# The variance of differential attention outputs by float32 products, and a second buffer for the second map's exponentials

## The chip, the cores and the metric

One core of one Trainium2 chip runs the whole kernel in one launch. The core has five queues that matter here: TensorE (matrix products, in the trace PE, with its weight loads shown apart as PEld), VectorE (DVE), ScalarE (ACT), GpSimd (POOL) and the queue that issues most transfers (SP). The metric is device time in microseconds (us), the median over runs. Before the change three runs gave 897.48, 897.6 and 898.41 us, median 897.6.

## The reference, cut to what matters

The block takes 1024 tokens of width 1024. One RMS-normalised input feeds two attention branches; the change lies in the first, differential attention with 4 heads and two score maps per head:

```python
o_diff = causal_multimap_attention(dq, dk, dv, weights, DIFF_HEAD_DIM ** -0.5)   # weights = [1, -lam]
o_diff = rms_norm(o_diff, diff_subln[layer]) * (1.0 - lambda_init)
o_diff = o_diff.transpose(0, 2, 1, 3).reshape(b, s, DIFF_WIDTH)
o_diff = o_diff * jax.nn.silu(dgate)

def rms_norm(x, gain):
    y = xf * lax.rsqrt(jnp.mean(xf * xf, axis=-1, keepdims=True) + NORM_EPS)
    return y * gain
```

So each head's 128 output values of a token are divided by the root of their mean square. That mean square is the variance of the title. The second branch (MLA, multi-head latent attention) has one score map per head; both branches are projected, gated, added, projected again and normalised.

## The kernel before, in words

All matrix products of the projections and of attention are done in three products of split operands (`mm3`, lines 159 to 162: high by high, high by low, low by high), each 512 columns wide where it can be. The work runs in five stages: the input products into values and latents (to about 130 us), the differential heads with the gate projections mixed in (130 to 574 us), a handover in which the MLA heads are prepared (574 to 600 us), MLA attention (to about 725 us), and the output products (to the end).

A differential head goes through two groups of four query blocks (`diff_head`, line 684). For each block `diff_scores` (line 608) makes two score tiles on TensorE (line 619); `softmax` (line 433) finds the row maximum on VectorE (line 435) and takes the exponential with its sum on ScalarE (line 438), the first map into tile `e0` to `e7`, the second into tile `eb`. `combine` (line 623) then weighs and subtracts the second map on VectorE (line 627). `eb` has one buffer, so the next block's second exponential may not start before line 627 has read the last one.

`values` (line 446) transposes the probabilities on TensorE, splits them, and gathers `ov`, a tile with the head's 128 values on the partitions and 512 tokens along the row. `diff_norm` (line 630) runs once for each group, 8 times in all:

- ScalarE squares `ov` into the float32 tile `sq` (line 632; its buffer has the tag `rt1`, and traces show it as `rt`).
- VectorE splits `sq` into three bfloat16 parts by four instructions (lines 642 to 645), and makes the gated, unnormalised output `o` (line 646).
- `variance` (line 648) makes the sum over the partitions on TensorE: for each 128 tokens three products with `parts` as the weights and `meanw`, two columns of 1/128, as the moving operand (line 652). That is 12 loads of weights and 12 products for each group, 96 in all.
- VectorE adds the epsilon (`ve`, line 654), GpSimd takes the power -1/2 (`rv`, line 656), and `diag` and `finish` spread the result over the partitions by two more products (lines 671, 672), multiply and store it.

In the last group (head 3, second half) the tiles `parts`, `o` and the diagonals lie in `e4` to `e7`, since that group falls into the handover. There TensorE works on the rope part of the MLA queries (two groups of nine products with `wqnh`) and on the MLA values (eight groups of six products with `wvh`). Each of these groups fills one of two `mm` PSUM buffers in turn: a query group's is free again when VectorE has read it twice (`rotate`, lines 487 and 488; 489 and 490 go on in SBUF), a value group's when ScalarE has copied it (`mvh`) and VectorE has written the remainder (`mvl`, line 153). `q_stack` (lines 493 to 498) then splits the rotated queries into `mqs` on ScalarE (line 496) and VectorE (line 498).

The order in the queues has two sources. The Python code issues filler work between the steps (`fill`, `defer`), and when the program is built a scheduler places each engine's instructions by priority and readiness; waits between engines are then added. Within a queue an instruction that waits holds all behind it.

Of the kernel before, what the change touches and what calls it, by code (L numbers as in the profile page):

```python
# [14 lines left out]
F32 = mybir.dt.float32  # L15
F32R = mybir.dt.float32r
BF16 = mybir.dt.bfloat16
I32 = mybir.dt.int32
AF = mybir.ActivationFunctionType
ALU = mybir.AluOpType  # L20
# [3 lines left out]
P = 128  # L24
S = 1024
# [26 lines left out]
def emit(tc, a):  # L52
    nc = tc.nc
    V, A, G, T = nc.vector, nc.scalar, nc.gpsimd, nc.tensor

    def pool(name, side=None, space=None, bufs=1):
        kw = {}
        if side:
            kw["side"] = side
        if space is not None:  # L60
            kw["space"] = space
        return tc.alloc_tile_pool(name=name, bufs=bufs, reuse_waits="tile", **kw) if space is not DRAM \
            else tc.alloc_tile_pool(name=name, bufs=bufs, **kw)
# [3 lines left out]
    def nm(s):  # L67
        counter[0] += 1
        return f"{s}_{counter[0]}"

    def mk(p, shape, dt, tag, bufs=None):
        return p.tile(shape, dt, name=nm(tag), tag=tag, bufs=bufs)

    def one(p, shape, dt, name):
        return p.tile(shape, dt, name=name, tag=name, bufs=1)
# [9 lines left out]
    def tick(ns):  # L85
        clock[0] += ns
        while later and clock[0] >= later[0][0]:
            heapq.heappop(later)[2]()
# [35 lines left out]
    const = pool("const", "left")  # L124
# [12 lines left out]
    ones = one(const, [P, P], F32, "ones")  # L137
    onesr = one(const, [P, P], F32R, "onesr")
    ident = one(const, [P, P], F32, "ident")
    meanw = one(const, [P, 2], BF16, "meanw")  # L140
    nhalf = one(const, [P, NB], F32, "nhalf")
    halfpi = one(const, [P, 1], F32, "halfpi")
    rstd = one(const, [P, NB], F32, "rstd")
# [23 lines left out]
    def blk(b):  # L167
        return slice(b * P, b * P + P)
# [233 lines left out]
    wk = pool("wk", "left")  # L402
# [15 lines left out]
    def chunks(W):  # L418
        if W == 640:
            return [(0, 384), (384, 256)]  # L420
        out, c = [], 0
        while c < W:
            n = min(512, max(256, W - c))
            out.append((c, n))
            c += n
        return out

    def scores_tile(W):

        sc = mk(ps, [P, S], F32, "sc", 2)  # L430
        return sc[:, P:S] if W == 640 else sc

    def softmax(sc, W, scale, dst):
        mn = mk(wk, [P, 1], F32, "mn", 4)
        V.tensor_tensor_reduce(sc[:, 0:W], sc[:, 0:W], mask[:, S - W:S], scale=-scale, scalar=BIG,  # L435
                               op0=ALU.add, op1=ALU.min, accum_out=mn)
        sm = mk(wk, [P, 1], F32, "sm", 8)
        A.activation(dst, sc[:, 0:W], AF.Exp, scale=-1.0, bias=mn, accum_out=sm)  # L438
        return sm

    def recip(sm):
        r = mk(wk, [P, 1], F32, "rs", 8)
        V.reciprocal(r, sm)  # L443
        return r
# [60 lines left out]
    later_pools = {}  # L505
# [102 lines left out]
    def diff_scores(h, i):  # L608
        qh, ql, kh, kl = stacks[h]
        W = (i + 1) * P  # L610
        ea = mk(wk, [P, W], F32, f"e{i}", 1)
        eb = mk(later_pools["st"], [P, S], F32, "eb", 1)
        sc = [scores_tile(W) for m in range(2)]

        for c0, n in chunks(W):
            for x, (q, k) in enumerate(((qh, kh), (qh, kl), (ql, kh))):
                for m in range(2):
                    r = slice(64 * m, 64 * m + 64)
                    T.matmul(sc[m][:, c0:c0 + n], lhsT=q[r, blk(i)], rhs=k[r, c0:c0 + n], start=x == 0, stop=x == 2)  # L619
            tick(3 * n * ROW)  # L620
        sums = [softmax(sc[m], W, DIFF_SCALE, e[:, 0:W]) for m, e in enumerate((ea, eb))]

        def combine():
            r1, r2 = recip(sums[0]), recip(sums[1])
            V.tensor_scalar(r2, r2, nlam, None, op0=ALU.mult)
            V.tensor_scalar(ea, ea, r1, None, op0=ALU.mult)
            V.scalar_tensor_tensor(ea, eb[:, 0:W], r2, ea, op0=ALU.mult, op1=ALU.add)
        return ea, combine

    def diff_norm(h, g, ov):  # L630
        sq = mk(wk, [P, 512], F32, "rt1", 2)
        A.activation(sq, ov, AF.Square)
        if (h, g) != (3, 1):
            parts = [mk(p1c, [P, 512], BF16, f"sq{i}", 1) for i in range(3)]
            o = mk(p1c, [P, 512], F32, "o", 1)
            dg = [mk(p1c, [P, 512], F32R, x, 1) for x in ("rt1r", "rt2r")]
        else:
            spare = [mk(wk, [P, (i + 1) * P], F32, f"e{i}", 1) for i in range(4, 8)]
            parts = spare[3].bitcast(BF16)
            parts = [parts[:, 512 * i:512 * i + 512] for i in range(3)]  # L640
            o, dg = spare[0][:, 0:512], [x[:, 0:512].bitcast(F32R) for x in spare[1:3]]
        V.tensor_copy(parts[0], sq)
        V.tensor_tensor(sq, sq, parts[0], op=ALU.subtract)
        V.tensor_copy(parts[1], sq)
        V.tensor_tensor(parts[2], sq, parts[1], op=ALU.subtract)
        V.scalar_tensor_tensor(o, ov, gsub, dgate[h, g], op0=ALU.mult, op1=ALU.mult)

        def variance():
            vb = bank_n()
            for j in range(4):  # L650
                for i in range(3):
                    T.matmul(vb[:, 2 * j:2 * j + 2], lhsT=parts[i][:, blk(j)], rhs=meanw, start=i == 0, stop=i == 2)
            ve = mk(wk, [P, 8], F32, "ve", 2)
            V.tensor_scalar(ve, vb[:, 0:8], EPS, None, op0=ALU.add)
            rv = mk(wk, [P, 4], F32, "rv", 2)
            G.tensor_tensor(rv, ve.rearrange("p (a b) -> p a b", b=2)[:, :, 0], nhalf[:, 0:4], op=ALU.pow)
            defer(2500, lambda: diag(rv))

        def diag(rv):
            rh = mk(wk, [P, 4], F32R, "rvh", 2)  # L660
            rl = mk(wk, [P, 4], F32R, "rvl", 2)
            V.tensor_copy(rh, rv)
            V.tensor_tensor(rl, rv, f32(rh), op=ALU.subtract)
            for x, t in zip((rh, rl), dg):
                (V if (h, g) == (3, 1) and t is dg[1] else G).tensor_tensor(t.rearrange("p (a b) -> p a b", b=P), ident.unsqueeze(1).broadcast_to([P, 4, P]),
                                f32(x).unsqueeze(2).broadcast_to([P, 4, P]), op=ALU.mult)
            defer(6000, finish)

        def finish():
            bb = bank_n()  # L670
            T.matmul(bb, lhsT=onesr, rhs=dg[0], start=True, stop=False)
            T.matmul(bb, lhsT=onesr, rhs=dg[1], start=False, stop=True)
            V.tensor_tensor(o, o, bb, op=ALU.mult)
            nc.sync.dma_start(d_od[h][:, half(g)], o)

        defer(6000, variance)
# [4 lines left out]
    def bank_n():  # L681
        return mk(ps, [P, 512], F32, "tp", 1)
# [130 lines left out]
    p1c = later_pools["c"]  # L813
# [179 lines left out]
    parts = {}  # L993
# [169 lines left out]
    for i, c in enumerate(quarters):  # L1163
# [8 lines left out]
        else:  # L1172
            sq = mk(p3d, [P, 256], F32, "sq3", 1)
# [86 lines left out]
```

## Time and profile before

| | |
|---|---|
| median of three runs | 897.6 us (897.48 to 898.41) |
| the profiled execution: its time, its span | 896.13 us, 894.4 us |
| TensorE busy | 874.7 us, 98% of the span |
| VectorE, ScalarE, GpSimd busy | 538.5, 335.5, 219.5 us |
| TensorE's mean granted clock | 0.995 of full speed |

The span is the stretch from the first to the last instruction; 1.7 us of the execution lie around it. A busy share of 98% on TensorE is not work at its peak: products are pipelined, their recorded ends overlap the next start, and a product of two columns counts as busy for 163 ns. What an operation costs TensorE is therefore read from start to start.

### The profile page before, as it was taken

The page shows a single profiled execution, that of the slowest core. Times are in us where ns is not written, and L with a number is a line of the kernel's source. Part 1 is how long each engine was busy: PE and PEld are TensorE (multiplying, and loading weights), DVE is VectorE, ACT ScalarE, POOL GpSimd, SP SyncE. Part 2 cuts the span into 40 slices and gives each one's busy share as a digit, 9 for nine tenths or more (in the row PEclk, how much of TensorE's full clock was granted, in tenths as well). Part 3 has the DMA queues.
Part 4 walks back from the last instruction along what each step waited for, and adds up shares of the span by engine and source line. Part 5 has one row for each costly group of instructions (what it writes and reads, how often), then busy time and mean ns, then how long its engine had stood idle before and what let it go on. Part 6 is the DMA issues. An engine that isn't in the chain of part 4 may idle for free.

```text
span 894.4 us, 11691 instructions
## 1 busy us (share of the span) xinstructions
PE 874.7 (98%) x4368; PEld 716.0 (80%) x4368; DVE 538.5 (60%) x1023; ACT 335.5 (38%) x654; POOL 219.5 (25%) x163
## 2 busy tenths in 40 slices
PE   9989999999999999999999999999999999999997
PEld 6879988787887878878778778778877788888886
DVE  5472348738368483784856755786676775561432
ACT  5651361334323343233422333745455542221211
POOL 2432013222223222322223131622313212210001
PEclk9998999999999999999999999999999999999999
DMA  8765026122131222222211215410104655434151
GB/s 294 289 192 161 23 87 220 48 71 80 62 107 59 76 90 64 91 71 82 72 59 33 95 31 185 161 34 25 48 25 154 200 178 187 141 102 146 58 178 47
DMA packets 48824, 96.71 MB, mean 108 GB/s; under 512 B 4992, under 2 KB 17536, under 8 KB 48768
## 3 DMA queue, kind: packets, MB, share of 16 engines
q1 hardware_dynamic: 46176, 89.81, 30.4%
q0 software_dynamic: 1152, 3.67, 1.3%
q10 hardware_dynamic: 1440, 2.49, 0.8%
q8 instruction: 34, 0.56, 0.3%
q14 instruction: 22, 0.18, 0.1%
HBM read 68.96 MB, written 27.00 MB: 107 GB/s over the span
## 4 chain that ended last, share of the span: by engine, by line
PE 85%; DVE 4%; DMA 4%; issue 2%; ACT 2%; POOL 1%; SPq 1%; POOLq 0%; DVEq 0%; ACTq 0%
PE mm L160 18%; PE mm L162 17%; PE mm L161 17%; PE sc L619 4%; PE acc L160 3%; PE acc L161 3%; PE acc L162 3%; PE tp L457 2%; PE bank L161 2%; PE bank L160 2%; PE bank L162 2%; PE pv L161 2%; PE pv L160 2%; PE pv L162 1%; PE sc L898 1%
## 5 line engine op out<-in xcount | busy, mean ns | idle before, releaser
L160 PE MATMUL mm<-hh,wh 128*128 128x512 f32 x512 | 205.9, 402 | 0.0
L162 PE MATMUL mm<-hh,wl 128*128 128x512 f32 x512 | 200.2, 391 | 0.0
L161 PE MATMUL mm<-hl,wh 128*128 128x512 f32 x512 | 199.9, 390 | 0.0
L153 POOL TENSOR_TENSOR wl<-wr,wh 128x1024 fp32r<-128x1024 f32 x32 | 81.8, 2558 | 240.2 <-ACT wh L152 240.2
L160 PEld LDWEIGHTS mm<-hh,wh 128*128 128x128 f32 x512 | 96.2, 188 | 25.0 <-issue 3.8
L162 PEld LDWEIGHTS mm<-hh,wl 128*128 128x128 f32 x512 | 96.1, 188 | 21.2
L161 PEld LDWEIGHTS mm<-hl,wh 128*128 128x128 f32 x512 | 96.3, 188 | 17.9
L438 ACT ACTIVATE e<-sc,mn 128x128 f32<-128x128 f32 (+3 forms) x64 | 47.5, 743 | 82.9 <-DVE mn L435 80.0
L435 DVE CUSTOM_DVE_ANT_0 sc<-sc,mask 128x128 f32<-128x128 f32 (+7 forms) x96 | 71.7, 774 | 10.1 <-PE sc L902 8.7
L153 DVE TENSOR_TENSOR pl<-tp,ph 128x512 fp32r<-128x512 f32 (+2 forms) x52 | 31.5, 606 | 62.2 <-ACT ph L152 62.2
L152 ACT CAST ph<-tp 128x512 fp32r<-128x512 f32 (+2 forms) x52 | 27.0, 520 | 84.7 <-PE tp L457 84.2
L160 PE MATMUL acc<-woh,mh 128*128 128x512 f32 (+1 forms) x136 | 51.7, 380 | 0.0
L162 PE MATMUL acc<-woh,ml 128*128 128x512 f32 (+1 forms) x136 | 51.7, 380 | 0.0
L161 PE MATMUL acc<-wol,mh 128*128 128x512 f32 (+1 forms) x136 | 51.7, 380 | 0.0
L152 ACT CAST wh<-wr 128x1024 fp32r<-128x1024 f32 x32 | 33.6, 1050 | 39.0 <-PE mm L161 28.6
L160 PE MATMUL bank<-wch,hh 128*128 128x384 f32 (+1 forms) x128 | 42.7, 335 | 3.8 <-ACT wch L152 3.8
L911 POOL TENSOR_TENSOR e<-e,rs 128x128 f32<-128x128 f32 (+5 forms) x24 | 24.9, 1042 | 73.5 <-DVE rs L443 73.4
L161 PE MATMUL bank<-wcl,hh 128*128 128x384 f32 (+1 forms) x128 | 42.6, 333 | 0.3 <-DVE wcl L153 0.3
L569 DVE TENSOR_TENSOR g<-mm,rbc 128x512 f32<-128x512 f32 x40 | 27.5, 688 | 25.5 <-PE mm L162 25.0
L162 PE MATMUL bank<-wch,hl 128*128 128x384 f32 (+1 forms) x128 | 42.4, 331 | 0.0
L153 POOL TENSOR_TENSOR wpl<-wpr,wph 128x512 fp32r<-128x512 f32 x16 | 22.0, 1377 | 68.0 <-ACT wph L152 68.0
L572 ACT ACTIVATE u<-g 128x512 f32<-128x512 f32 x40 | 25.2, 630 | 20.3 <-DVE g L569 15.4
(291 smaller groups left out, 1859.0 us busy)
## 6 DMA issues: line engine op xcount, KB each, us to landing
wr<-in_w_t SPq DMA_DIRECT2D x32, 512.0 KB, 3.5
d_t<-u SPq DMA_DIRECT2D x32, 256.0 KB, 2.0
tg<-d_t SPq DMA_DIRECT2D x32, 256.0 KB, 3.0
big<-in_x SPq DMA_DIRECT2D x8, 512.0 KB, 8.3
wor<-in_w_out SPq DMA_DIRECT2D x8, 512.0 KB, 4.5
xres<-in_x SPq DMA_DIRECT2D x8, 512.0 KB, 5.1
big<-in_xT SPq DMA_DIRECT2D x7, 512.0 KB, 6.6
craw<-d_c SPq DMA_DIRECT2D x5, 512.0 KB, 6.0
```

The lines of the kernel that those rows point to most:

```text
L152: A.copy(hi, src)
L153: (eng or V).tensor_tensor(lo, src, f32(hi), op=ALU.subtract)
L160: T.matmul(ps, lhsT=lh, rhs=rh, start=first, stop=False)
L161: T.matmul(ps, lhsT=lh, rhs=rl, start=False, stop=False)
L162: T.matmul(ps, lhsT=ll, rhs=rh, start=False, stop=last)
L435: V.tensor_tensor_reduce(sc[:, 0:W], sc[:, 0:W], mask[:, S - W:S], scale=-scale, scalar=BIG, op0=ALU.add, op1=ALU.min, accum_out=mn)
L438: A.activation(dst, sc[:, 0:W], AF.Exp, scale=-1.0, bias=mn, accum_out=sm)
L457: T.transpose(tp[:, blk(j)], probs[j][:, blk(kb)], ident)
L569: V.tensor_tensor(g, b, rbc[:, half(n)], op=ALU.mult)
L572: A.activation(u, g, AF.Tanh, scale=0.5 / by)
L619: T.matmul(sc[m][:, c0:c0 + n], lhsT=q[r, blk(i)], rhs=k[r, c0:c0 + n], start=x == 0, stop=x == 2)
L911: G.tensor_tensor(e, e, r.broadcast_to([P, W]), op=ALU.mult)
```

## The change

The squares go to TensorE as they are, in float32. For each 128 tokens one float32 product takes the place of three bfloat16 products, `meanw` becomes a float32 tile, and the four splitting instructions and their tiles are gone. Besides, `eb` gets a second buffer.

```diff
-    meanw = one(const, [P, 2], BF16, "meanw")
+    meanw = one(const, [P, 2], F32, "meanw")
...
     ea = mk(wk, [P, W], F32, f"e{i}", 1)
-    eb = mk(later_pools["st"], [P, S], F32, "eb", 1)
+    eb = mk(later_pools["st"], [P, S], F32, "eb", 2)
...
     A.activation(sq, ov, AF.Square)
     if (h, g) != (3, 1):
-            parts = [mk(p1c, [P, 512], BF16, f"sq{i}", 1) for i in range(3)]
             o = mk(p1c, [P, 512], F32, "o", 1)
             dg = [mk(p1c, [P, 512], F32R, x, 1) for x in ("rt1r", "rt2r")]
         else:
-            spare = [mk(wk, [P, (i + 1) * P], F32, f"e{i}", 1) for i in range(4, 8)]
-            parts = spare[3].bitcast(BF16)
-            parts = [parts[:, 512 * i:512 * i + 512] for i in range(3)]
+            spare = [mk(wk, [P, (i + 1) * P], F32, f"e{i}", 1) for i in range(4, 7)]
             o, dg = spare[0][:, 0:512], [x[:, 0:512].bitcast(F32R) for x in spare[1:3]]
-        V.tensor_copy(parts[0], sq)
-        V.tensor_tensor(sq, sq, parts[0], op=ALU.subtract)
-        V.tensor_copy(parts[1], sq)
-        V.tensor_tensor(parts[2], sq, parts[1], op=ALU.subtract)
         V.scalar_tensor_tensor(o, ov, gsub, dgate[h, g], op0=ALU.mult, op1=ALU.mult)

         def variance():
             vb = bank_n()
             for j in range(4):
-                for i in range(3):
-                    T.matmul(vb[:, 2 * j:2 * j + 2], lhsT=parts[i][:, blk(j)], rhs=meanw, start=i == 0, stop=i == 2)
+                T.matmul(vb[:, 2 * j:2 * j + 2], lhsT=sq[:, blk(j)], rhs=meanw, start=True, stop=True)
```

On TensorE, in the first head's sixth block of scores, before (three of the twelve products; `sc` are the score tiles, `tp` the PSUM tile of the variance):

```order
L619 MATMUL sc_1967<-kh_1421,ql_1420 128x512
L652 LDWEIGHTS sq_337_1899
L652 MATMUL tp_1974<-meanw,sq_337_1899 128x2
L652 LDWEIGHTS sq_338_1900
L652 MATMUL tp_1974<-meanw,sq_338_1900 128x2
L652 LDWEIGHTS sq_339_1901
L652 MATMUL tp_1974<-meanw,sq_339_1901 128x2
```

and now (`rt` is the tile of squares; a float32 product loads its weights itself and has no row for it):

```order
L619 MATMUL sc_1959<-kh_1421,ql_1420 128x512
L619 MATMUL sc_1960<-kh_1421,ql_1420 128x512
L644 MATMUL tp_1967<-meanw,rt_336_1897 128x2 x4
L619 MATMUL sc_1959<-kh_1421,qh_1419 128x256
L619 MATMUL sc_1960<-kh_1421,qh_1419 128x256
```

The place among the neighbours is the same, here and in the other six groups before the handover; twelve loads and products became four instructions.

On VectorE in the handover, before (`e` and `rt` the parts and the squares, `rt` with `mm` the rotated queries, `mvl` the remainders of MLA values, `ve` the variance with epsilon):

```order
L643 TENSOR_TENSOR rt_1116_5328<-rt_1116_5328,e_1120_5333 128x512
L487 STREAM_SHUFFLE rt_1132_5398<-mm_5387 128x512
L644 CAST e_1120_5333<-rt_1116_5328 128x512
L488 TENSOR_TENSOR rt_1131_5397<-mm_5387,cosm 128x512
L645 TENSOR_TENSOR e_1120_5333<-rt_1116_5328,e_1120_5333 128x512
L489 TENSOR_TENSOR rt_1132_5398<-rt_1132_5398,sinm 128x512
L153 TENSOR_TENSOR mvl_5352<-mm_5407,mvh_5345 128x512
L490 TENSOR_TENSOR rt_1131_5397<-rt_1131_5397,rt_1132_5398 128x512
L153 TENSOR_TENSOR mvl_5353<-mm_5416,mvh_5346 128x512
L654 TENSOR_SCALAR ve_5458<-tp_5445 128x8
L498 TENSOR_TENSOR mqs_1128_5385<-rt_1131_5397,mqs_1128_5385 64x512
L498 TENSOR_TENSOR mqs_1129_5386<-rt_1131_5397,mqs_1129_5386 64x512
```

and now (`rvh` is the rounded result of GpSimd's power; the lines after the diff's are 7 or 8 lower than before):

```order
L639 SCALAR_TENSOR_TENSOR e_1096_5225<-pv_5022,gsub,du_4390 128x512
L487 STREAM_SHUFFLE rt_1110_5288<-mm_5277 128x512
L488 TENSOR_TENSOR rt_1109_5287<-mm_5277,cosm 128x512
L489 TENSOR_TENSOR rt_1110_5288<-rt_1110_5288,sinm 128x512
L646 TENSOR_SCALAR ve_5340<-tp_5335 128x8
L490 TENSOR_TENSOR rt_1109_5287<-rt_1109_5287,rt_1110_5288 128x512
L153 TENSOR_TENSOR mvl_5242<-mm_5297,mvh_5235 128x512
L654 CAST rvh_5363<-rv_5342 128x4
L498 TENSOR_TENSOR mqs_1106_5275<-rt_1109_5287,mqs_1106_5275 64x512
L498 TENSOR_TENSOR mqs_1107_5276<-rt_1109_5287,mqs_1107_5276 64x512
L153 TENSOR_TENSOR mvl_5243<-mm_5306,mvh_5236 128x512
L655 TENSOR_TENSOR rvl_5364<-rv_5342,rvh_5363 128x4
```

The splitting is gone from between the rotation's steps, `ve` and `rvh` moved forward, and the second `mvl` moved back behind `rvh` and both `mqs`.

On GpSimd, ahead of the heads, the scheduler now puts the first two loads of the differential values (lines 603, 604) ahead of one split of weights (line 153); on SP the two loads of line 605 stand ahead of a store and a load that they followed before.

## Rows read from the trace of the kernel before

**Rows 1.** The page: busy us of each engine, its share and its instructions.

```profile
PE 874.7 (98%) x4368; PEld 716.0 (80%) x4368; DVE 538.5 (60%) x1023; ACT 335.5 (38%) x654; POOL 219.5 (25%) x163
```

**Rows 2.** TensorE's waits, 130 to 574 us, then 574 to 598 us (total, times, longest).

```profile
PE tp L457 <- DVE pl L153: 1.4, 1, 1.4
...
PE mm L160 <- DVE mvl L153: 1.5, 1, 1.5
PE tp L672 <- DVE e L665: 0.5, 1, 0.5
```

**Rows 3.** Durations by line in ns (min/median/max): variance, then the last float32 product.

```profile
L652 PEld LDWEIGHTS <-sq x84: 95/96/100, 209.1 to 529.5; 128*128 128x128 bf16 x84
L474 PEld LDWEIGHTS pv<-plast,dvf x16: 187/188/192, 200.9 to 574.1; 128*128 128x128 f32 x16
L474 PE MATMUL pv<-plast,dvf x16: 270/273/274, 201.1 to 574.2; 128*128 128x128 f32 x16
```

**Rows 4.** Timeline of TensorE, a group between scores (start us, us; xN merges N).

```profile
209.08 0.45 PE L652 MATMUL tp<-meanw,sq 128*128 128x2 bf16 x12
209.46 0.39 PE L619 MATMUL sc<-kh,qh 64*128 64x256 f32 x2
```

**Rows 5.** Timeline of TensorE, a group between products of a projection.

```profile
263.14 0.39 PE L162 MATMUL mm<-hh,wl 128*128 128x512 f32 x1
263.37 0.45 PE L652 MATMUL tp<-meanw,sq 128*128 128x2 bf16 x12
263.68 0.48 PE L160 MATMUL mm<-hh,wh 128*128 128x512 f32 x1
264.01 0.39 PE L161 MATMUL mm<-hl,wh 128*128 128x512 f32 x1
```

**Rows 6.** Timeline of TensorE, one float32 product between products of a projection.

```profile
256.10 0.40 PE L162 MATMUL mm<-hh,wl 128*128 128x512 f32 x1
256.33 0.39 PE L474 MATMUL pv<-plast,dvf 128*128 128x128 f32 x2
256.79 0.39 PE L161 MATMUL mm<-hl,wh 128*128 128x512 f32 x1
```

**Rows 7.** Tile eb: ScalarE's idle time before its exponentials (us, times).

```profile
  DVE mn L435: 0.8, 4
```

**Rows 8.** Timeline of the handover, all engines.

```profile
576.14 0.40 PE L162 MATMUL mm<-ch,wqnl 128*128 128x512 f32 x1
577.90 3.23 POOL L153 TENSOR_TENSOR krl<-u,krh 128x512 fp32r<-128x512 f32 x2
578.83 1.17 DVE L645 TENSOR_TENSOR e<-rt,e 128x512 bf16<-128x512 f32 x1
579.93 1.76 DVE L489 TENSOR_TENSOR rt<-rt,sinm 128x512 f32<-128x512 f32 x1
581.61 0.68 DVE L153 TENSOR_TENSOR mvl<-mm,mvh 128x512 fp32r<-128x512 f32 x1
582.34 0.50 PE L160 MATMUL mm<-ch,wqnh 128*128 128x512 f32 x1 [1.49 <-DVE mvl L153]
582.98 1.26 ACT L496 CAST mqs<-rt 64x512 fp32r<-64x512 f32 x2 [1.74 <-DVE rt L490]
583.63 1.41 DVE L498 TENSOR_TENSOR mqs<-rt,mqs 64x512 fp32r<-64x512 f32 x2
583.64 1.54 POOL L656 TENSOR_TENSOR rv<-ve,nhalf 128x4 f32<-128x4 f32 x1 [2.50 <-DVE ve L654]
...
597.53 0.49 PE L457 MATMUL mm<-ident,e 128*128 128x128 f32 x3
```

**Rows 9.** Line 489 by itself: ns of one (min/median/max).

```profile
L489 DVE TENSOR_TENSOR rt<-rt,srs x16: 677/682/2655, 144.4 to 484.0; 128x512 f32<-128x512 f32 x16
```

**Rows 10.** Timeline of GpSimd and of the SP queue ahead of the heads.

```profile
138.10 0.32 SPq L528 DMA_DIRECT2D d_c<-rt  x1
138.35 2.40 POOL L153 TENSOR_TENSOR wl<-wr,wh 128x1024 fp32r<-128x1024 f32 x1 [14.82 <-ACT wh L152]
```

## The prediction, made before the changed kernel ran

> **What bounds the kernel now.** I read the busy shares first: TensorE is busy for 874.7 of 894.4 us, VectorE for 538.5 [rows 1]. A change that takes work off VectorE is thus worth only what TensorE waits for VectorE, and a change that adds to TensorE is paid in full where nothing holds TensorE up. So the second view is TensorE's own waits, by stage. From 130 to 574 us, where seven of the eight variance groups lie, it waits for VectorE once, 1.4 us, for the remainder of a transposed tile (line 153) and not for the variance; in the handover it waits 1.5 us for the remainder `mvl` and 0.5 us for a diagonal [rows 2]. Third, the timeline of TensorE around a variance group, from start to start, because the recorded busy time of so short products overlaps.
>
> **What the group of products costs now.** Between scores, the twelve bfloat16 loads and products begin at 209.08 and the next score product at 209.46: 0.38 us [rows 4]. Between products of a projection, 0.87 us pass from the start at 263.14 to the start at 264.01 [rows 5]; two products of 512 columns lie in it, each 0.23 us by the step from 256.10 to 256.33 [rows 6], so the group costs 0.87 - 0.46 = 0.41 us. That is 0.03 us for each of the twelve.
>
> **What it costs after.** Four float32 products with two columns never ran in this trace, but a float32 product with 128 columns did, line 474. It is written as one product for each of 8 groups, and the trace has 16 loads and 16 products for these [rows 3]: each float32 product is two passes, each with its own load. In a stream of projection products the two passes cost 0.69 us from 256.10 to 256.79 less 0.46, so 0.23 us, or 0.115 us for a pass [rows 6]. The load of float32 weights is recorded with 188 ns against 95 for bfloat16 [rows 3]: it is the load, twice as long, that a product of two columns cannot cover. The four products are eight passes: 8 x 0.115 = 0.92 us. The price from both sides: if a pass were as short as the bfloat16 ones now, 8 x 0.03 = 0.24 us; if load and product did not overlap at all, 188 + 273 ns for a pass [rows 3], 3.7 us. I take 0.115, the row of the same kind of operand. It adds 0.92 - 0.41 = 0.51 us to each of three groups that lie between projection products and 0.92 - 0.38 = 0.54 us to each of four between scores (rows 4 and 5 show one of each; the others repeat them): 1.53 + 2.16 = 3.7 us. Nothing covers this: TensorE has no wait there that the longer group could fall into.
>
> The row has two passes. By the Trainium skill, FP8 and Floating Point Precision, section TensorE Precision Notes, a true float32 product takes four passes through the array. By two loads for each the sum stays 3.7 us; with four loads it is the third rival below, and the sixteen records speak for two.
>
> **What VectorE's relief is worth.** Four instructions go from each group. In the seven groups before the handover VectorE's next work only starts earlier, TensorE does not wait for it, and I price that at nothing; the cover is TensorE's own stream, and the one wait of 1.4 us lies in the values of a head, far behind the variance. Both ends: none of it goes (0), or all (-1.4 us).
>
> **Second buffer for `eb`.** ScalarE's idle time before all exponentials into `eb` is 0.8 us, and what ended it was the row minimum, not the reader of `eb` [rows 7]. The wait that the buffer removes was never the last one. Price 0.
>
> **The moved loads.** On GpSimd two of the issues of lines 603 and 604 now stand ahead of a split that began at 138.35, after 14.82 us of idleness, when ScalarE released it; what they wait for, products on tables ahead of the heads, is done well before, so they fall into that idle stretch [rows 10]. On SP the two loads of line 605 fall ahead of the store at 138.10, which waits for VectorE anyway [rows 10]. Price 0; if one of them did hold SP up, a load of weights behind it would be late, at most the length of a few issues of 0.3 us.
>
> **The handover, step by step.** Here VectorE is the engine waited for, so I follow the new order. Before, the second query group of TensorE began at 582.34 after 1.49 us of waiting for `mvl`, which ran at 581.61 because four splitting instructions stood between the steps of the rotation and two instructions were stretched: line 645 took 1.17 us, line 489 1.76 [rows 8], where line 489 has a median of 0.68 [rows 9]. Both began while GpSimd's two subtractions into `krl` (577.90 to 581.13) ran, and ended about 0.55 us after one of these [rows 8]. So two operands in SBUF on VectorE wait for GpSimd's subtraction to end. The Trainium skill, SBUF — State Buffer, section Who interferes with whom, states just this as a lock held for a whole instruction; the trace agrees, and without it the second query group would start some 0.8 us earlier in what follows.
>
> After: the first query group's last product starts at 576.14 and takes 0.40 [rows 8], so the shuffle starts at about 576.6, with line 643 no longer ahead of it; with 0.68 us an instruction line 489 starts near 577.9 and runs into the `krl` pair, and 490 follows that pair's end. I let the pair end between 580.4 (VectorE less in its way) and 581.1 as now, and 490 at 581.0; then `mvl` ends at 581.65 and the second query group starts at 581.7. TensorE by itself would be ready at 580.9 (from 576.14: seven products at 0.23, eight passes, six scores of 256 columns at half of 0.23, six more products, and 0.2 for changes of operand): a wait of 0.8 in place of 1.5. But now the second `mvl` stands behind `rvh` and both `mqs`. ScalarE's pair takes 1.26 us from 581.05, VectorE's pair 1.41 after it [rows 8], so that `mvl` ends at 584.4, while TensorE wants its buffer at 583.8, nine products later: a new wait of 0.65. `rvh` needs GpSimd's power (up to 1.54 us [rows 8]), done by about 582.2, and is not last. The same pattern holds the fourth `mvl` behind the next pair: a new wait of 1.0. The second diagonal is made early, and its 0.5 us go with the restart behind it. From 584.5 on TensorE has six value groups at 1.4, fourteen scores for 2.5 and two diagonals for 0.5, in all 11.2, with the wait of 1.0 and 0.4 for changes of operand: the first transposes of MLA start at 597.1 against 597.53 [rows 8]. That is -0.4 us, with the longer variance group in it. If all three waits vanished it would be -2.9; if each is as long again, +2.0.
>
> **The sum.** +3.7 - 0.4 = +3.3 us on the profiled execution, 896.13 (span 894.4 and 1.7 around it) to 899.4. The median of the runs is 897.6, 1.5 above that execution; the same step gives 900.9 us. Less than 0.2%, 1.8 us, a measurement of this kernel hardly tells from no change.
>
> **Rivals.**
> 1. The handover gives back what the groups cost: all three waits of mine vanish, -2.9, net +0.8, 898.4 us. For it: the waits hang on tenths of a microsecond on VectorE and GpSimd. Against: the second `mvl` does stand behind two `mqs` in the new order, and 1.41 us is a firm row.
> 2. Faster, by the price of a short pass. If a load hides behind the neighbouring product and a pass takes the 0.03 us of the bfloat16 ones, the groups save 0.17 x 3 + 0.14 x 4 = 1.1 us, the handover another 0.7 on top of its 0.4: -2.2, 895.4 us. It decides at 0.058 us for a pass: there 3 x 0.41 + 4 x 0.38 + 0.4 = 56 passes. For it: twelve loads become eight. Against: no float32 load of 128 columns in these rows follows another closer than 0.11 us, and the longer recorded load. The Trainium skill, TensorE: Matmul & The Clock Gate, section Weight-path perf modes, gives the fast weight load only to types other than FP32, which speaks against this rival too.
> 3. Four loads for a float32 product, the rule named above: 16 x 0.115 = 1.84 us a group, +1.43 x 3 + 1.46 x 4 = 10.1, and 0.9 more in the handover: +10.6, 908.2 us. Against: 16 records for 8 products [rows 3].
> 4. A stretched wait between VectorE and GpSimd, like line 489's 2.66 us at most [rows 9], appears or goes elsewhere: 1 to 2 us either way, for which no place can be named; it widens the range.
>
> **Chances.** My forecast 0.66, with a range of its own of 899.3 to 902.8 (the handover from -2.0 to +1.5); rival 1 0.18; rival 2 0.08; rival 3 0.05; 0.03 for others. Slower by over 0.2% (above 899.4): 0.61 of the forecast's 0.66, and rival 3: 0.66. Within 0.2%: rival 1, 0.05 from the forecast's low end and a little of the others: 0.25. Faster: rival 2 and a stall that happens to go, 0.09. The range that should hold 8 times in 10 goes from 897.8, in the middle of rival 1, to 903.4, which leaves out rivals 2 and 3.
>
> **What would show it.** Line 644's four products should show 8 loads of about 188 ns and 8 products in a group, and 0.9 us from the start of the first to the next product in the seven groups; 0.3 would be rival 2, 1.8 rival 3. ScalarE's exponentials into `eb` should be released by the row minimum as before. In the handover TensorE should wait for `mvl` two or three times, and the MLA transposes start some 3.3 us later than before (597.53 + 3.7 - 0.4). The forecast is wrong if the seven groups cost what they cost now, or if that point comes no later than before.

## The result, and the profile after

The changed kernel takes 903.9 us (median; 901.8 to 905.3) against 897.5 us for the kernel before on the same chip: ratio 1.0068, 95% interval 1.0046 to 1.0090, slower by 6.4 us. Measured again later (`after_again`, below) the ratio was 1.0062 (1.0042 to 1.0082). I had forecast 900.9 us, +3.3, and a range up to 903.4. The direction is as forecast, the size is not. Two runs of the experiments below, one of `f32r_sq` (1073 us at a mean granted clock of 0.75) and one of `last_one_eb` (2211 us), are slow ones and stand in no ratio.

The profiled execution took 905.27 us (span 903.6). Its page, the line that answers to [rows 1], engine by engine busy us, share and instructions:

```profile
PE 880.4 (97%) x4336; PEld 721.9 (80%) x4336; DVE 525.3 (58%) x991; ACT 335.4 (37%) x654; POOL 216.2 (24%) x163
```

VectorE lost 13 us of work and TensorE gained 6, part of that in the start (below). TensorE's waits, first from 130 us to the handover, then in the handover (engine, line, what it waited for: total, times, longest), answering to [rows 2]:

```profile
PE tp L457 <- DVE pl L153: 1.4, 1, 1.4
PE pv L522 <- ACT rt L525: 0.3, 1, 0.3
...
PE mm L160 <- DVE mvl L153: 1.5, 2, 1.0
PE sc L890 <- ACT e L438: 1.3, 1, 1.3
```

As long as the seven groups run, TensorE waits only where it did before (the profile of before has both of the first two lines as well); in the handover there are three waits in place of two, 2.8 us in place of 2.0. The durations of the variance products (min/median/max in ns), answering to [rows 3]:

```profile
L644 PEld LDWEIGHTS tp<-meanw,rt x64: 187/192/192, 212.0 to 585.2; 128*128 128x128 f32 x64
L644 PE MATMUL tp<-meanw,rt x64: 165/251/272, 212.0 to 585.2; 128*128 128x2 f32 x64
```

64 loads and 64 products for 32 float32 products: two recorded passes each, with a load of 192 ns (median) where the price had 188. TensorE's timeline around a group between scores and one between products of a projection, answering to [rows 4, 5]:

```profile
211.97 1.05 PE L644 MATMUL tp<-meanw,rt 128*128 128x2 f32 x8
212.95 0.39 PE L619 MATMUL sc<-kh,qh 64*128 64x256 f32 x2
...
266.63 0.39 PE L162 MATMUL mm<-hh,wl 128*128 128x512 f32 x1
266.86 0.95 PE L644 MATMUL tp<-meanw,rt 128*128 128x2 f32 x8
267.67 0.49 PE L160 MATMUL mm<-hh,wh 128*128 128x512 f32 x1
267.99 0.40 PE L161 MATMUL mm<-hl,wh 128*128 128x512 f32 x1
```

From 266.63 to 267.99 pass 1.36 us, less 0.46 for the two products of 512 columns: 0.90 us for eight passes (forecast 0.92). Between scores the group takes 0.98 us where twelve bfloat16 products took 0.38. All seven groups repeat one of these two: 3 x 0.49 + 4 x 0.60 = 3.87 us more.

To see where the rest went I took each product of TensorE that both kernels have, and the difference of its start times (each counted from the first product of its trace). This table, worked out from the two timelines, gives how much a kernel lost (+) or gained against the profile of before in each stretch of that profile, in us. What the experiments gave is in it already; the first row is the changed kernel.

```
stretch (us)     0-76  76-205 205-574 574-600 600-690 690-760 760-888
changed kernel   2.85    0.04    3.90    0.57    0.03    1.76    0.00
after_again     -2.58    0.04    3.90    0.60    0.07    2.33    0.00
f32_one_eb      -0.75    0.00    3.89    0.63    0.05    2.01    0.00
seven_same      -1.60    0.00    3.90    0.12   -0.02    1.34    0.00
f32_seven       -0.57    0.07    3.82    0.11    0.13    2.24   -1.62
last_same       -0.38    0.02    0.00    0.64    0.05    0.86    0.00
f32_last_only   -3.58    0.03   -0.18    0.65    0.12    0.46   -1.62
last_one_eb     -1.23    0.01   -0.13    0.63    0.16    0.64   -1.62
f32r_look       -0.29   -0.04    0.66    0.59    0.08    0.50    0.00
two_eb          -0.86   -0.03   -0.01    1.89    0.00    0.49    0.00
pad             -1.42   -0.02   -0.02   -0.01    0.11    1.73   -1.62
end_shift       -1.43    0.00    0.00   -0.01    0.06   -0.39   -1.65
twice           -1.43    0.00    2.11    0.73    0.02    1.09    0.00
twice_b         -1.49    0.03    2.09    0.05    0.10    1.21    0.00
lump            -1.85   -0.03    4.54    0.77   -0.01    0.98    0.00
lump_b          -1.18    0.04    5.91    1.96   -0.01    1.89    0.00
```

Four places move: the start, the seven groups (205 to 574), the handover (574 to 600) and a stretch from 690 to 760 us, the end of MLA's attention and the first output products. The start is chance: 2.85 late in one profile of the changed kernel, 2.58 early in the other, with no instruction there that the change touches except the type of one constant. In the fifteen other rows the start is 0.29 to 3.58 us shorter than in the profile of before. The late one began with a longer wait for the first split of the input, the last field here:

```profile
7.58 2.92 PE L160 MATMUL bank<-wdh,hh 128*128 128x512 f32 x6 [1.76 <-ACT hh L156]
```

where the profile of before shows 0.39 us of waiting:

```profile
6.16 1.81 PE L160 MATMUL bank<-wdh,hh 128*128 128x512 f32 x6 [0.39 <-ACT hh L156]
```

And near 70 us, after TensorE has waited for weights, the granted clock comes back at different times. The changed kernel's first profile by stretch (busy us and instructions of TensorE, its loads, VectorE, ScalarE, GpSimd; then the granted clock, DMA share, GB/s), and its second:

```profile
66.00:70.00 4.00, 0.67 (x2) 0.41 (x3) 1.35 (x3) 3.10 (x5) 1.26 (x1) 0.88 0.97 283
70.00:74.00 4.00, 4.00 (x13) 4.00 (x14) 1.46 (x3) 0.56 (x2) 0.64 (x1) 0.50 0.96 288
```

```profile
66.00:70.00 4.00, 4.00 (x17) 4.00 (x16) 1.41 (x3) 0.33 (x1) 0.86 (x1) 0.62 0.96 281
70.00:74.00 4.00, 4.00 (x24) 4.00 (x24) 0.66 (x1) 0.51 (x1) 4.00 (x3) 1.00 1.00 351
```

At 0.50, the lower of the two levels (1.2 GHz), 13 products pass in 4 us, at 1.00 (2.4 GHz) 24.

### The profile page after: what moved, and what is told of

Read it like the earlier page. It is cut to its first block, busy times and chain, and to the rows that moved or that the text cites. A ratio compares the mean times of both kernels' runs of the same rounds, so it can differ in the third digit from the quotient of the medians.

```text
span 903.6 us, 11589 instructions
## 1 busy us (share of the span) xinstructions
PE 880.4 (97%) x4336; PEld 721.9 (80%) x4336; DVE 525.3 (58%) x991; ACT 335.4 (37%) x654; POOL 216.2 (24%) x163
## 4 chain that ended last, share of the span: by engine, by line
PE 82%; DMA 7%; DVE 5%; ACT 2%; issue 2%; POOL 2%; SPq 0%; POOLq 0%; DVEq 0%; ACTq 0%
PE mm L160 17%; PE mm L162 16%; PE mm L161 16%; PE sc L619 4%; PE acc L160 3%; PE acc L162 3%; PE acc L161 3%; PE tp L457 2%; PE bank L161 2%; DMA big<-in_xT 2%; PE bank L160 2%; PE bank L162 2%; PE pv L161 2%; PE pv L160 1%; PE pv L162 1%
```

## The experiments

Ratios are to the kernel before on the same chip (896.4 to 897.2 us there), with 95% intervals; they are those on record, and differ by up to 0.0013 from the quotients of the medians (`after_again`: 900.9 / 896.5 = 1.0049). Float32 "in seven" means the groups ahead of the handover, "in the last" the group of head 3 in the handover.

| run | what differs from the kernel before | median us | ratio |
|---|---|---|---|
| two_eb | second place for `eb` | 895.8 | 0.9986 (0.9971-1.0002) |
| f32_one_eb | float32 in all, one `eb` | 902.0 | 1.0056 (1.0038-1.0075) |
| f32r_sq | as changed, float32r | 897.3 | 1.0001 (0.9982-1.0019) |
| f32_last_only | float32 in the last, two `eb`, tiles moved | 894.3 | 0.9972 (0.9955-0.9989) |
| last_one_eb | the same, one `eb` | 894.9 | 0.9965 (0.9948-0.9982) |
| f32_seven | float32 in seven, tiles moved | 899.8 | 1.0019 (1.0004-1.0034) |
| pad | one unused constant, tiles moved | 893.7 | 0.9953 (0.9937-0.9969) |
| after_again | the changed kernel | 900.9 | 1.0062 (1.0042-1.0082) |
| seven_same | float32 in seven, nothing moved | 900.3 | 1.0052 (1.0034-1.0069) |
| last_same | float32 in the last, nothing moved | 896.1 | 0.9998 (0.9985-1.0011) |
| end_shift | ten late weight tiles moved | 894.6 | 0.9989 (0.9975-1.0002) |
| twice | bfloat16 products of the seven twice | 899.2 | 1.0023 (1.0006-1.0040) |
| lump | first group's products eleven times | 900.6 | 1.0040 (1.0025-1.0054) |

f32r_look, twice_b and lump_b ran once each, for their profiles: 897.6, 898.1 and 904.7 us.

**The parts of the edit apart, first attempt.**

```diff
 two_eb (on the kernel before)
-        eb = mk(later_pools["st"], [P, S], F32, "eb", 1)
+        eb = mk(later_pools["st"], [P, S], F32, "eb", 2)
 f32_one_eb (on the changed kernel): the same line back to 1
```

> The kernel before with one edit: two places for `eb`. The order of instructions on every engine stays as before. Theory A (the float32 groups cost about 3.9 us, the new order from the handover on the rest, and the late start of the profiled run is chance): no change, 897.5 us within 0.2%. Theory B (the other 2.5 us of the 6.4 come from the second place, by where tiles now lie in memory or by what it lets ScalarE do earlier): 899.5 to 900.5 us.

> The changed kernel with one place for `eb` again, so the float32 variance alone; the order on every engine is that of the changed kernel. Theory A: as the changed kernel, 903.9 us within 1 us, and ScalarE's exponentials into `eb` are again released by the row minimum. Theory B: 2 to 3 us less, 901 to 902 us.

No place of `eb` is worth anything that can be measured: two_eb lies within 0.3% (theory B asked for 2 to 3 us more, it took 0.6 less) and its seven-group stretch moved by 0.01 us. With one place the changed kernel is still slower by 0.56%; its 902.0 us lie at theory B's upper end and outside theory A's 1 us, but the kernel before ran 1.1 us faster there than where these times were set, and the ratio cannot be told from the changed kernel's 1.0062. Theory B falls for `eb` by two_eb.

```diff
 f32r_sq, f32r_look (on the changed kernel)
-    meanw = one(const, [P, 2], F32, "meanw")
+    meanw = one(const, [P, 2], F32R, "meanw")
...
-    V.memset(meanw, 1.0 / P)
+    V.tensor_scalar(meanw, ones[:, 0:2], 1.0 / P, None, op0=ALU.mult)
...
-        sq = mk(wk, [P, 512], F32, "rt1", 2)
+        sq = mk(wk, [P, 512], F32, "rt1", 2).bitcast(F32R)
```

> The changed kernel with the squares and the column of 1/128 written as float32r in place of float32, so that each of the four products is one load and one product; the squares lose their lowest bits. The order of TensorE, ScalarE, GpSimd and SP is that of the changed kernel. Theory A: a pass costs between 0.06 and 0.115 us, a group 0.24 to 0.46 us where bfloat16 took 0.38 to 0.41, so the seven groups give -1.1 to +0.4 us against the kernel before, and what is left is the new order from the handover on, about +2: 898.4 to 900 us. Theory C (the groups' steps are only shifted waits, and the order and the start carry the loss): 902 us or more.

> The kernel with float32r squares once more, for its profile alone: the time of a group of four loads and four products on TensorE, from start to start. 0.24 to 0.46 us; if it is 0.4, the seven groups cost what the bfloat16 parts cost, which is what the timed runs (no difference from the kernel before) suggest.

The loss is gone (1.0001), with everything else of the change in place. Theory C falls here; theory A's 898.4 to 900 us were too high, since the 2 us that it left for the new order do not show. The groups, by the same views as above:

```profile
L644 PEld LDWEIGHTS tp<-meanw,rt x32: 187/190/192, 208.7 to 578.3; 128*128 128x128 f32 x32
L644 PE MATMUL tp<-meanw,rt x32: 166/250/271, 208.7 to 578.3; 128*128 128x2 f32 x32
```

```profile
262.93 0.39 PE L162 MATMUL mm<-hh,wl 128*128 128x512 f32 x1
263.16 0.50 PE L644 MATMUL tp<-meanw,rt 128*128 128x2 f32 x4
263.52 0.49 PE L160 MATMUL mm<-hh,wh 128*128 128x512 f32 x1
263.84 0.40 PE L161 MATMUL mm<-hl,wh 128*128 128x512 f32 x1
```

Four loads, and 0.91 - 0.46 = 0.45 us a group: 0.113 us a pass, what a pass of float32 takes in the same place (0.90 / 8). Between scores it is 0.54 us against 0.98. It is the number of passes that costs.

f32_last_only, on the changed kernel, has both forms of the variance; f32_seven has `==` for `!=`, and last_one_eb also one place for `eb`.

```diff
+    meanb = one(const, [P, 2], BF16, "meanb")
...
+        three = (h, g) != (3, 1)
...
+        if three:
+            V.tensor_copy(parts[0], sq)
...
+                for i in range(3 if three else 1):
+                    if three:
+                        T.matmul(vb[:, 2 * j:2 * j + 2], lhsT=parts[i][:, blk(j)], rhs=meanb, start=i == 0, stop=i == 2)
...
```

> The changed kernel with the seven groups ahead of the handover in three bfloat16 parts again, and only the last group, of head 3, in float32. Theory A: without the seven groups' 3.9 us, the handover and what follows cost 0.5 to 2.5 us: 898 to 900 us, and in the profile TensorE's lead over the kernel before is lost between 574 and 745 us alone. Theory C: 902 us or more, as the changed kernel. If the handover gave back 0.4 us as I predicted: 897 us.

> Float32 in the last group alone, as in the run before with that name's pattern (seven groups in bfloat16 parts), and one place for `eb` in place of two. It tells whether the 2 us that the float32 last group gained there come from the new order in the handover or from the second place. Theory H (the new order gains): again 1 to 3 us under the kernel before. Theory E (the second place does it): 0 within 0.2%. In the profile the waits of the new handover should be the same three as in the changed kernel: 1.0 and 0.5 us for `mvl`, 1.3 us for `e`.

> The changed kernel with the last group, of head 3, in three bfloat16 parts again, and the seven groups ahead of it in float32: the old order in the handover, the long groups and the moved loads. Theory A: seven times 0.5 to 0.6 us, 4.1 us (0.46%) over the kernel before; if the old handover is the worse one, up to 6 us. Theory C (the handover and what follows carry the loss): below 2 us.

These seemed to say that the last group in float32 gains 2 to 3 us, against theories A and C and my own forecast of its first run, and that the seven groups cost 1.7 us, which is theory C's "below 2 us". The suspicion fell on `meanb`, a constant more that moves the tiles behind it, so it was tried by itself:

```diff
 pad (on the kernel before)
+    spare_c = one(const, [P, 2], F32, "spare_c")
...
+    V.memset(spare_c, 1.0 / P)
```

> The kernel before with one more constant tile of two float32 columns, set once and never read. Nothing else changes, so it measures how far two kernels with the same work differ, and what a shifted layout does to the start. Theory A (no part of the loss is placement): 0 within 0.2%, and a second profile of the old handover, which should begin MLA's transposes 0 to 2 us later than in the profile of the kernel before, against the variance's start. Theory B (a shift of a few bytes makes the first 75 us faster or slower): more than 0.2% from the kernel before, and that difference lies ahead of 130 us in the profile.

An unused constant makes the kernel 0.47% faster, which neither theory had: theory A allowed 0.2%, theory B looked for it ahead of 130 us. So the three runs above carry a gain of their own, of which the column 760-888 shows 1.62 us; against `pad`, on its chip, the last group (`last_one_eb`) costs 1.2 us and the seven 6.2. (The section on the hardware comes back to it.) The same edits with both constants in the place of one, so that no tile behind them moves:

```diff
 seven_same, last_same (here against f32_seven, f32_last_only)
-    meanw = one(const, [P, 2], F32, "meanw")
-    meanb = one(const, [P, 2], BF16, "meanb")
+    means = one(const, [P, 4], F32, "means")
+    meanw, meanb = means[:, 0:2], means[:, 2:3].bitcast(BF16)
```

> The changed kernel once more, on the chip of the next two, and its second profile. Theory S (the change's parts add up): 4.5 to 6.5 us over the kernel before; the late start of its first profile (2.7 us behind by 8 us) does not come back, the seven groups again take 3.9 us, the handover again loses 0.5 to 0.6, and the rest falls behind 690 us. If the late start belongs to the change, it is there again.

> Float32 in the seven groups ahead of the handover, three bfloat16 parts in the last group, and both constants in the place of one, so that no other tile moves. Theory S: 4 us (0.45%) over the kernel before, up to 5 if the waits of MLA's attention come out longer. Theory I (the loss of the whole comes mostly from the handover or from what the handover triggers): at most 2 us.

> Float32 in the last group alone, three bfloat16 parts in the seven others, and no other tile moved. Theory S: 0 to 1.5 us over the kernel before, with MLA's transposes 0.5 us later against the variance's start of the last group, by the same three waits as in the changed kernel. My prediction's step says -0.4 us. If the 2 us that this edit seemed to gain before belong to the order and not to the moved tiles, it is 2 us faster here too.

Theory S stands: +0.52% for the seven groups, nothing measurable for the last one, +0.62% for both, on one chip. The late start of the first profile did not come back. The loss is in the main that of the seven groups, with what they bring behind 690 us: theory I (at most 2 us; the interval is 3.0 to 6.2) and theory C fall.

**The late loss, 690 to 760 us.** Still open was why a stretch far behind the change lost 1.3 to 2.3 us in every profile with the seven groups in float32.

```diff
 twice (on the kernel before); lump: 11 if (h, g) == (0, 0) else 1
-                for i in range(3):
+                for i in list(range(3)) * (1 if (h, g) == (3, 1) else 2):
                     T.matmul(vb[:, 2 * j:2 * j + 2], lhsT=parts[i][:, blk(j)], rhs=meanw, start=i == 0, stop=i == 2)
```

> The kernel before with the twelve bfloat16 products of each of the seven groups issued twice, the second time over the first, so that a group takes some 0.38 us more on TensorE and nothing else changes (the result is the same). Theory T (whatever delays TensorE in the seven groups also draws a longer wait in MLA's attention, as the float32 groups did): 2.7 us in the groups and 1 to 2 us more between 690 and 760 us, 3.7 to 4.7 over the kernel before. Theory U (the wait there is only where the loads of `omr` happen to land): 2.7 us, and the stretch from 690 to 760 us within -0.4 to 0.9 us of the profile before, as in the runs without float32 in the seven groups.

> The kernel with the products issued twice, once more for a second profile: theory T 1 to 2 us lost between 690 and 760 us again, theory U some other value from -0.4 to 0.9.

> The kernel before with the twelve products of the first group alone issued eleven times, so that TensorE is some 3.6 us later from 209 us on and the other six groups stay as they are. Theory T in the form that a later TensorE is enough: 3.6 us and 1 to 2 more between 690 and 760 us. In the form that each group must be longer, or by theory U: 3.6 us alone.

> The kernel with the first group's products issued eleven times, once more for a second profile: the same two answers as for its first.

`twice` cost 2.1 us in the groups, 0.30 us each where both theories had 0.38, and 2.1 us when timed (interval 0.5 to 3.6), which agrees with TensorE's added time being paid in full there. The lump cost more than I had priced, 4.5 and 5.9 us, in two profiles of one kernel. Its 120 more products took 3.0 us; behind them the granted clock fell, though TensorE had not been idle:

```profile
207.00:210.60 3.60, 3.60 (x138) 3.40 (x134) 0.00 (x0) 0.00 (x0) 0.00 (x0) 1.00 0.09 31
210.60:214.00 3.40, 3.40 (x14) 2.69 (x13) 2.14 (x6) 0.68 (x1) 2.80 (x3) 0.50 0.00 0
```

At 0.50 the projection's products came 0.43 us apart in place of 0.23, and in `lump_b` this lasted longer.

From 690 to 760 us these four profiles lost 0.98 to 1.90 us: theory T's 1 to 2, not theory U's. But `pad`, without a longer group, lost 1.73, so single profiles of this stretch decide nothing. Split by place, the stretch has three waits. Two lie in MLA's attention, where TensorE waits for `ph`. The second of them in the changed kernel (SP's queue, ScalarE, TensorE):

```profile
715.64 3.24 SPq L1050 DMA_DIRECT2D omr<-d_om  x3
...
720.91 1.96 ACT L152 CAST omh<-omr 128x512 fp32r<-128x512 f32 x3 [3.44 <-DMA omr<-d_om]
...
722.77 0.58 ACT L152 CAST ph<-mm 128x512 fp32r<-128x512 f32 x1
...
723.40 0.51 PE L160 MATMUL pv<-ph,mvh 128*128 128x512 f32 x1 [1.59 <-ACT ph L152]
```

and the same place before:

```profile
708.21 1.27 SPq L1058 DMA_DIRECT2D omr<-d_om  x3
...
711.78 0.62 ACT L152 CAST omh<-omr 128x512 fp32r<-128x512 f32 x1 [1.74 <-DMA omr<-d_om]
...
714.30 0.58 ACT L152 CAST ph<-mm 128x512 fp32r<-128x512 f32 x1
...
714.93 0.51 PE L160 MATMUL pv<-ph,mvh 128*128 128x512 f32 x1 [0.54 <-ACT ph L152]
```

ScalarE's cast of `omr`, a tile read back from memory, stands ahead of `ph` in its queue; when the load lands late (the cast began 5.3 us after its issue here, 3.6 before), TensorE waits for `ph`. That is 1.05 us of the changed kernel's 1.76. The other 0.7 lie in the output products, where VectorE waits for `tg`, another tile read back, and TensorE's next products for VectorE; now and before:

```profile
747.03 0.69 DVE L1009 SCALAR_TENSOR_TENSOR tg<-tg,mm 128x512 f32<-128x512 f32 x1 [2.09 <-DMA tg<-d_t]
```

```profile
737.36 0.69 DVE L1017 SCALAR_TENSOR_TENSOR tg<-tg,mm 128x512 f32<-128x512 f32 x1 [1.17 <-DMA tg<-d_t]
```

The mean loss against the profile of before, from the same timelines:

```
profiles                                      attention  output products  together
float32 in the seven groups (5)                   1.16             0.78      1.94
no longer groups (8, before's own 0 with them)    0.42             0.12      0.54
groups lengthened otherwise (4)                   1.12             0.18      1.30
```

So the profile of before was on the lucky side by 0.5 us, and 1.4 us come with float32 in the seven groups. Half of that lies in the attention, where the kernels lengthened otherwise lose as much; half in the output products, where only one of those loses anything (`lump_b`, 0.68 at another wait).

The traces show one thing that sets the five profiles apart. A DMA queue of kind `instruction`, q8, moves a packet of 16 KB for about every 257 of TensorE's loads and products (34 packets for 8736 of them before); the changed kernel has 64 fewer, so the packets fall at other places of the program. In all five profiles one lies in the flight of the first of these `omr` loads and the next one in that of the `tg` load, and the loads landed 4.4 to 5.2 and 4.8 to 5.2 us after their issue. In the twelve others neither load has one beside it, and they landed after 2.8 to 3.6 and 3.5 to 4.4 us. No run moved these packets alone, so that they delay the loads is a reading and not shown.

## Why the prediction was off

**The groups: right.** 3.90 us measured in 205-574, in four profiles of the same layout to 0.01 us; forecast 3.7. The third rival fails: 64 loads for 32 products and 0.90 us a group are two loads a product, not four and 1.84. The Trainium skill (FP8 and Floating Point Precision, TensorE Precision Notes) has four passes; the records show two, each at the price of the single pass of float32r (0.113 us). Rival 2 fails too: a pass did not hide its load.

**VectorE's relief, `eb`, the moved loads: right, 0.** The stretch 76-205, where the moved loads lie, changed by 0.04 us; 205-574 is the same with one and two places for `eb`. The 0.8 us for which ScalarE sat idle before its exponentials into `eb` are still there in `two_eb` and gone in `f32_one_eb`: VectorE's relief took them away, not the second place, and TensorE got nothing of it.

**The handover: wrong by 1 us.** Forecast -0.4, measured +0.57 to +0.65 in seven profiles with the new order. The mechanism was there, in these lines of the changed kernel that answer to [rows 8]:

```profile
583.98 2.98 POOL L153 TENSOR_TENSOR krl<-u,krh 128x512 fp32r<-128x512 f32 x2
...
585.84 1.66 DVE L490 TENSOR_TENSOR rt<-rt,rt 128x512 f32<-128x512 f32 x1
...
587.42 0.68 DVE L153 TENSOR_TENSOR mvl<-mm,mvh 128x512 fp32r<-128x512 f32 x1
...
588.16 0.50 PE L160 MATMUL mm<-ch,wqnh 128*128 128x512 f32 x1 [0.49 <-DVE mvl L153]
...
588.60 2.14 DVE L498 TENSOR_TENSOR mqs<-rt,mqs 64x512 fp32r<-64x512 f32 x2
588.71 1.47 POOL L657 TENSOR_TENSOR e<-ident,rvh 128x512 fp32r<-128x512 f32 x1 [0.35 <-DVE rvh L654]
...
590.77 0.69 DVE L153 TENSOR_TENSOR mvl<-mm,mvh 128x512 fp32r<-128x512 f32 x1
...
591.51 0.50 PE L160 MATMUL mm<-wvh,ch 128*128 128x512 f32 x1 [1.01 <-DVE mvl L153]
...
598.50 0.44 PE L890 MATMUL sc<-knh,qnh 128*128 128x384 f32 x1 [1.31 <-ACT e L438]
...
604.90 0.49 PE L457 MATMUL mm<-ident,e 128*128 128x128 f32 x3
```

Line 490 was stretched by the `krl` pair as forecast. The wait for the first `mvl` was 0.49 us, not 0.8. I had missed that GpSimd's first diagonal (line 657) would run beside the `mqs` remainders and stretch them from 1.41 to 2.14 us, so the second `mvl` cost 1.01 in place of 0.65. The third wait was not at the fourth `mvl`, where I had 1.0; it came later, 1.31, for the exponentials behind the last `mqs` in ScalarE's queue. TensorE's products behind the second wait took 0.5 us more than I had summed, 0.2 of it by a slip: my terms (8.4, 2.5 and 0.5) make 11.4, not 11.2. (A second slip changes nothing: the price of a pass that decides rival 2 is 3.15 / 56 = 0.056 us, not 0.058.) Taking off the 6.79 us of delay at the entry, the transposes start at 598.1, not 597.1.

Of the old handover I had one profile, and it was a good one. Nine more old-order profiles give 0 to 0.1 us five times and 0.7 to 2.0 four times, as in `two_eb`, where line 643 met the `krl` pair and TensorE waited in the variance group itself:

```profile
576.47 2.96 POOL L153 TENSOR_TENSOR krl<-u,krh 128x512 fp32r<-128x512 f32 x2
576.50 1.81 DVE L643 TENSOR_TENSOR rt<-rt,e 128x512 f32<-128x512 f32 x1
...
578.86 0.85 DVE L644 CAST e<-rt 128x512 bf16<-128x512 f32 x1
...
579.77 0.18 PE L652 MATMUL tp<-meanw,e 128*128 128x2 bf16 x1 [2.18 <-DVE e L644]
```

In `two_eb` and `lump_b`, the two that lost 1.9, the granted clock also fell to its lower level behind that wait of over 2 us (`two_eb`: 0.50 from 580 to 582 us); in `twice` and `lump`, which lost 0.7 behind the same wait, it stayed at 1.00. On average, 0.56 us over ten, the old order costs what the new one costs without fail, 0.62, which fits last_same's 0.9998.

**The sum: the step that failed.** I let it end with MLA's transposes, as if all behind them only moved, and so priced the waits for the read-back tiles at nothing without a reason. Against the one profile of before, the parts are 3.90 + 0.6 + 1.76 or 2.33 (690-760) = 6.2 to 6.8. Against the average of the profiles they are 3.90 + 0.06 + 1.4 = 5.4 us. Measured: 6.4 and 5.6 (4.4 by the medians), with intervals of 2 us to either side. Of the 2.1 us by which 5.4 exceeds my +3.3, 0.2 is the groups, 0.5 the handover and 1.4 the stretch from 690 to 760 us. That the first four runs came out 0.5 us above my range is in part chance, as their interval starts at +4.1 us; that the sum lacked these terms is not. Why the loads land later with float32 in the seven groups stays open; the place of the q8 packets is the one lead.

## What to carry to other kernels

On a saturated TensorE count the passes of a small product, not its instructions: eight float32 passes with 128 columns of weights cost 0.9 us, four of float32r 0.45, twelve of bfloat16 0.4 (between scores 0.98, 0.54 and 0.38), and VectorE's relief is worth nothing where TensorE does not wait for it. Before a stall in one profile is used as a price, look whether it is a fixed wait or a lottery; two or three profiles of the same kernel tell. In a comparison of edits keep the tiles' places fixed: one constant more was worth as much as the edits under study.

## What the runs showed of the hardware, unexpected

The step from one 512-column product to the next depends on where the operands lie. `pad` and `end_shift` differ from the kernel before in this, the latter by

```diff
 end_shift (on the kernel before)
     wol += [one(p3d, [P, D], F32R, f"wol{k}") for k in range(EARLY, KD)]
+    one(p3d, [P, 8], F32, "gap8")
```

> The kernel before with 32 bytes of unused tile behind the late weights of the output projection, which moves these ten tiles by 32 bytes and nothing else. The kernel with one more constant was faster and took 226.7 ns where the kernel before takes 232.4 from one 512-column product to the next in the last 55 us. Theory M (the step depends on whether the two operands of a product lie alike in memory): 255 products of the output projection take 226.7 instead of 232.4 ns, 1.5 us less, and the first 60 us stay as before: 0.17% faster. Theory N (the gain of the kernel with one more constant came from its start): no difference.

The output projection of the kernel before, and of end_shift, each from one product to the 60th behind it:

```profile
843.24 0.40 PE L162 MATMUL acc<-woh,ml 128*128 128x512 f32 x1
...
857.15 0.40 PE L162 MATMUL acc<-woh,ml 128*128 128x512 f32 x1
```

```profile
839.99 0.39 PE L162 MATMUL acc<-woh,ml 128*128 128x512 f32 x1
...
853.59 0.39 PE L162 MATMUL acc<-woh,ml 128*128 128x512 f32 x1
```

13.91 us against 13.60, 231.8 ns against 226.7. In the built program of the kernel before, the ten late weight tiles begin at multiples of 64 bytes and `mh` and `ml` 32 bytes beyond one; with the gap both begin 32 beyond, with `pad` both at multiples. In `pad` it is the first projection whose operands no longer lie alike (`wdh` moved, `hh` did not), and there its step is 233.3 ns (20 to 50 us; 226.7 before), 0.9 us lost in 5 to 60 us. Like places gain 1.62 to 1.65 us in the last stretch in each of the five kernels that have them (theory M: 1.5). Timed, end_shift gained 0.11% (-0.02 to 0.25), not quite apart from nothing, and `pad` 0.47%, 4.2 us, which is more than a gain of 1.6 and a loss of 0.9 explain; the rest stays open, beside a start in which single profiles differ by 6 us. `pad` is the fastest version run, ahead of both kernels: 893.7 us.
